# S5's rows regrouped and its small products, with one level of a block inverse, as pairs of 64x64 quadrants, in a two-layer hybrid decoder on one Trainium2 core

## Chip, cores and metric

One NeuronCore of a Trainium2 chip runs the whole program. The metric is the device time of one execution in microseconds (us), lower is better; of the kernel before there are three runs and one execution taken by the profiler.

## What is computed

Two layers of a decoder trunk on 512 tokens of width 1024, in float32. Each layer has a half-step SwiGLU feed-forward, three token mixers side by side with one input and one output projection, and a second feed-forward, each between two RMS norms. The change touches the mixer S5 and the solution of the triangular systems of the two others.

```python
def s5_mix(u, a_re, a_im, log_dt, b_re, b_im, c_re, c_im, d_skip, w_glu, b_glu):
    ug = u.reshape(bsz, t_len, S5_GROUPS, S5_GROUP_DIM)          # 16 groups x 16 channels
    dt = jnp.exp(log_dt)[:, None]
    mag = jnp.exp(dt * a_re)
    ang = dt * a_im
    abar_re, abar_im = mag * jnp.cos(ang), mag * jnp.sin(ang)    # 16 groups x 64 states
    ...
    bu_re = jnp.einsum('btgh,gnh->btgn', ug, bbar_re)
    bu_im = jnp.einsum('btgh,gnh->btgn', ug, bbar_im)
    ...
    _, _, x_re, x_im = lax.associative_scan(_complex_linear_combine, elems, axis=1)
    y = (jnp.einsum('btgn,ghn->btgh', x_re, c_re) - jnp.einsum('btgn,ghn->btgh', x_im, c_im)
         + d_skip.reshape(S5_GROUPS, S5_GROUP_DIM) * ug)
    z = jax.nn.gelu(y.reshape(bsz, t_len, S5_WIDTH))
    return z * jax.nn.sigmoid(z @ w_glu + b_glu)
...
    sol = lax.linalg.triangular_solve(a_low + eye, rhs, left_side=True, lower=True, unit_diagonal=True)
```

## The kernel before

The sequence is cut into two halves of 256 tokens (`HALF`), and `run` goes through steps such as A00 (first feed-forward, layer 0, half 0), P00 (input projection), M00 (the mixers), O00 (output projection), B00 (second feed-forward). The steps overlap: a scheduler that simulates a timeline (`schedule_with_timeline_sim`) sets the order of the instructions on each engine, so small products of a mixer stand between the large ones of a feed-forward. Each engine works through its own list in order; loads and stores are all issued by SP.

The large products are made three times (`mm3`, lines 245 to 247), from a high and a low part of each weight: `raw` is loaded by SP (line 221), ScalarE makes `whi` (line 226), VectorE makes `wlo` (line 227). `ph` are the feed-forward's up products, `acc` its down products.

S5 works in blocks of four time steps. Of the 16 groups, two (g = 0, 1) share each of 8 pairs p. In `s5_setup` (once a layer) two powers-of-Abar tables are built: `Bx` (64 states of two groups on the 128 partitions, by step and channel) and `Q` (the same for C). As two groups share a row block, the entries of one group against the other are zeros: `Bx` and `Q` are set to zero by POOL, and POOL copies each group's block into place (lines 1192 and 1220). 16 transposes (`plv`, line 1207) turn `Bx`, 16 products (`pk5`, line 1238) form the response within a block of four steps, to which VectorE adds (line 1245). All of it goes to DRAM as `s5w`. `s5` (once per half and layer, four calls) writes its input to DRAM and reads it back as `U4` with rows in the order (step, channel of the pair) by one DMA (line 1259), forms v with 16 products of 128x128 weights and 64 columns (line 1271), runs the recurrence on VectorE, and forms y with 24 products (lines 1313 to 1315).

The two other mixers need the inverses of 16 triangular 128x128 matrices in each call, 8 in `AT` and 8 in `ATg`. `inverse` inverts their 32x32 diagonal blocks by a recurrence on VectorE. `inverse2` goes from 32 to 64 and from 64 to 128: at the first level 8 products `py` (line 610) and 8 products `pz` (line 618) for each of the two groups of matrices, full 128x128 weights and 64 columns, of which half of each output is masked off or meets zeros; 16 transposes (line 625) then bring the transposed result `W` up to date. At the second level the products already are single 64x64 quadrants (lines 632 and 639). An fp32 product stands as two records in the trace, a transpose or a `mm3` product as one.

The pools that the changed tiles use are `b1`, `b2` and `b4` in SBUF and two PSUM banks `mx`. RWKV's products at line 763 are the one place where two halves of the array's rows are used in turn:

```python
for j in range(2):
    for o in (1, 0):
        q = slice(64 * o, 64 * o + 64)
        m = nc.tensor.matmul(ps[o][:, j], a[q, j, c], ar[q, j, c], start=True, stop=True)
```

Of the kernel before, what the change touches and what calls it, by code (L numbers as in the profile page):

```python
# [12 lines left out]
F32 = mybir.dt.float32  # L13
# [3 lines left out]
AF = mybir.ActivationFunctionType  # L17
ALU = mybir.AluOpType
# [23 lines left out]
class Trunk:  # L42
# [52 lines left out]
    def constants(self):  # L95
# [18 lines left out]
        self.hind = self.band(2, 64, 64, 0, "hind")  # L114
        self.bd32 = self.band(4, 32, 32, 0, "bd32")
        self.m32 = self.band(2, 32, 64, 32, "m32")
# [13 lines left out]
    def params(self, l):  # L130
# [20 lines left out]
        for s in range(4):  # L151
            self.late(nc.sync.dma_start(out=rows[R_D:R_D + 8, 32 * s:32 * s + 32],
                                        in_=io["s5_d"][l].rearrange("(p q) -> p q", q=32)))
# [430 lines left out]
    def inverse2(self, ATs, X0):  # L584
# [8 lines left out]
        nc.vector.transpose(wc.rearrange("p n k -> p (n k)"), xc.rearrange("p n k -> p (n k)"))  # L593
        Xs, Ws = [], []
        for z in range(2):
            xb = self.b4([P, 8, 4, 32], "xb")
            nc.vector.tensor_tensor(xb, xc[:, 8 * z:8 * z + 8].unsqueeze(2).to_broadcast([P, 8, 4, 32]),
                              self.bd32.unsqueeze(1).unsqueeze(3).to_broadcast([P, 8, 4, 32]), ALU.mult)
            X = xb.rearrange("p h b k -> p h (b k)")
# [3 lines left out]
            Xs.append(X)  # L603
            Ws.append(W)

        Ys = []
        for z in range(2):
            py = self.mx([P, 8, 2, 32], "py")
# [6 lines left out]
        for z in range(2):  # L615
            pz = self.mx([P, 8, 2, 32], "pz")
# [502 lines left out]
    def s5_setup(self, l):  # L1119
# [58 lines left out]
        Pw = [(self.b1([P, 8, 16], "P0r"), self.b1([P, 8, 16], "P0i"))]  # L1178
        self.cmul(Pw[0][0], Pw[0][1], b16(cr), b16(ci), Bre, Bim, [P, 8, 16])
        Cc = []  # L1180
        for cl in L["C"]:
            pc = self.mx([P, P], "pc")
            nc.tensor.transpose(pc, cl.rearrange("p t n -> p (t n)"), self.ident)
            cc = self.b1([P, 8, 16], "cc")
            nc.vector.tensor_copy(cc.rearrange("p a b -> p (a b)"), pc)
            Cc.append(cc)
        W5 = self.s5w[l]

        Bx = [self.b4([P, 8, 4, 2, 16], "Bx") for _ in range(2)]
        for t in Bx:  # L1190
            self.late(nc.gpsimd.memset(t, 0.0))
        cp = lambda o, i: nc.gpsimd.tensor_scalar(o, i, 1.0, 0.0, ALU.mult, ALU.add)
        cur = Pw[0]
        for j in range(4):
            for z in range(2):
                for g in range(2):
                    q = slice(64 * g, 64 * g + 64)
                    cp(Bx[z][q, :, 3 - j, g], cur[z][q])
            if j < 3:
                nx = (self.b1([P, 8, 16], "Pr"), self.b1([P, 8, 16], "Pi"))  # L1200
                self.cmul(nx[0], nx[1], b16(abr), b16(abi), cur[0], cur[1], [P, 8, 16])
                cur = nx
        for z in range(2):
            for hp in range(2):
                pv = self.mx([P, 4, P], "plv")
                for p in range(4):
                    nc.tensor.transpose(pv[:, p], Bx[z][:, 4 * hp + p].rearrange("n s g c -> n (s g c)"), self.ident)
                lv = self.b2([P, 4, P], "lv")
                nc.scalar.activation(lv, pv, AF.Copy)
                nc.sync.dma_start(out=W5[:, 4 * hp:4 * hp + 4, z], in_=lv)  # L1210
        Q = [[self.b4([P, 4, 5, 32], "Q") for _ in range(2)] for _ in range(2)]
        for t in Q[0] + Q[1]:
            self.late(nc.gpsimd.memset(t, 0.0))
        cur = Cc
        for j in range(5):
            for z in range(2):
                for g in range(2):
                    q = slice(64 * g, 64 * g + 64)
                    for hp in range(2):
                        nc.gpsimd.tensor_scalar(Q[z][hp][q, :, j, 16 * g:16 * g + 16], cur[z][q, 4 * hp:4 * hp + 4],  # L1220
                                                1.0 - 2 * z, 0.0, ALU.mult, ALU.add)
            if j < 4:
                nx = (self.b1([P, 8, 16], "Qcr"), self.b1([P, 8, 16], "Qci"))
                self.cmul(nx[0], nx[1], b16(abr), b16(abi), cur[0], cur[1], [P, 8, 16])
                cur = nx
        for z in range(2):
            for hp in range(2):
                nc.sync.dma_start(out=W5[:, 4 * hp:4 * hp + 4, 2 + z], in_=Q[z][hp][:, :, 1:5].rearrange("n p j c -> n p (j c)"))

        for hp in range(2):  # L1230
            pk = self.mx([P, 4, P], "pk5")
            rep = [self.b2([P, 4, 4, 32], "rep") for _ in range(2)]
            for z in range(2):
                nc.scalar.activation(rep[z], Bx[z][:, 4 * hp:4 * hp + 4, 3].rearrange("n p g c -> n p (g c)").unsqueeze(2)
                                     .to_broadcast([P, 4, 4, 32]), AF.Copy)
            for p in range(4):
                for z in range(2):
                    nc.tensor.matmul(pk[:, p], rep[z][:, p].rearrange("n s c -> n (s c)"),
                                     Q[z][hp][:, p, 0:4].rearrange("n j c -> n (j c)"), start=z == 0, stop=z == 1)
            K = self.b2([P, 4, P], "K5")  # L1240
            nc.gpsimd.tensor_tensor(K, self.ident.unsqueeze(1).to_broadcast([P, 4, P]),
                                    pr[:, R_D + 4 * hp:R_D + 4 * hp + 4].unsqueeze(2).to_broadcast([P, 4, P]), ALU.mult)
            for s in range(4):
                q = slice(32 * s, 32 * s + 32)
                nc.vector.tensor_tensor(K[q, :, 32 * s:], K[q, :, 32 * s:], pk[q, :, 0:P - 32 * s], ALU.add)
            nc.sync.dma_start(out=W5[:, 4 * hp:4 * hp + 4, 4], in_=K)


    def s5(self, l, h, I, mixT):
# [3 lines left out]
        W5 = self.s5w[l]  # L1253
# [5 lines left out]
        nc.sync.dma_start(out=U4, in_=scr.rearrange("s q p c -> (s q) p c"))  # L1259
# [6 lines left out]
        for p2 in range(4):  # L1266
            lv = self.mw.tile([P, 2, 2, P], F32, tag="lv5", name=self.n("lv5"), bufs=4)
            self.after(nc.sync.dma_start(out=lv, in_=W5[:, 2 * p2:2 * p2 + 2, 0:2]), I["usi"])
            for p in range(2):
                for z in range(2):  # L1270
                    nc.tensor.matmul(pv[z][:, 2 * p2 + p], lv[:, p, z], U4[:, 2 * p2 + p], start=True, stop=True)
# [36 lines left out]
        for p2 in range(4):  # L1308
            lx = self.b4([P, 2, 3, P], "lx5")
            self.after(nc.sync.dma_start(out=lx, in_=W5[:, 2 * p2:2 * p2 + 2, 2:5]), scan)  # L1310
            for p in range(2):
                q = 2 * p2 + p
                nc.tensor.matmul(py[:, q], lx[:, p, 2], U4[:, q], start=True, stop=False)
                nc.tensor.matmul(py[:, q], lx[:, p, 0], X[0][:, q, 0:NC5], start=False, stop=False)
                nc.tensor.matmul(py[:, q], lx[:, p, 1], X[1][:, q, 0:NC5], start=False, stop=True)
# [203 lines left out]
```

## Time and profile before

| | us |
|---|---|
| runs (median of three) | 2262.53 (2256.43 to 2264.71) |
| profiled execution | 2262.76 |
| its span, first to last instruction | 2261.0 |
| TensorE busy | 2204.1 |
| VectorE busy | 1688.2 |
| ScalarE busy | 1191.7 |
| POOL busy | 163.2 |

The profile names engines PE (TensorE's products), PEld (its weight loads), DVE (VectorE), ACT (ScalarE), POOL, SP (which issues DMAs, SPq). L763 is line 763. A name such as `pk<-ar,ka` is output from inputs, and buffer numbers are left out. 64*128 behind a product are the rows and columns of the array that it uses.

### The profile page before, as it was taken

The page shows a single profiled execution, that of the slowest core. Times are in us where ns is not written, and L with a number is a line of the kernel's source. Part 1 is how long each engine was busy: PE and PEld are TensorE (multiplying, and loading weights), DVE is VectorE, ACT ScalarE, POOL GpSimd, SP SyncE. Part 2 cuts the span into 40 slices and gives each one's busy share as a digit, 9 for nine tenths or more (in the row PEclk, how much of TensorE's full clock was granted, in tenths as well). Part 3 has the DMA queues.
Part 4 walks back from the last instruction along what each step waited for, and adds up shares of the span by engine and source line. Part 5 has one row for each costly group of instructions (what it writes and reads, how often), then busy time and mean ns, then how long its engine had stood idle before and what let it go on. Part 6 is the DMA issues. An engine that isn't in the chain of part 4 may idle for free.

```text
span 2261.0 us, 44455 instructions
## 1 busy us (share of the span) xinstructions
PE 2204.1 (97%) x15800; PEld 2032.1 (90%) x15800; DVE 1688.2 (75%) x3779; ACT 1191.7 (53%) x2521; POOL 163.2 (7%) x372
## 2 busy tenths in 40 slices
PE   8999999999999999999999999999999899998998
PEld 7998999897979999799989999889979799997997
DVE  6697886867876967768776678878677878677665
ACT  5555764444744444555555557544456545455554
POOL 2032000001000001201300010000020000001000
PEclk9999999999999999999999999999999999999999
DMA  7776765654765744567656677556467556456665
GB/s 207 199 209 186 186 196 151 187 145 153 202 192 154 206 136 142 175 186 220 200 177 188 189 197 204 155 172 189 130 179 207 162 172 193 123 154 187 190 187 154
DMA packets 604963, 403.67 MB, mean 179 GB/s; under 512 B 63306, under 2 KB 534340, under 8 KB 604740
## 3 DMA queue, kind: packets, MB, share of 16 engines
q1 hardware_dynamic: 604740, 400.82, 61.3%
q8 instruction: 124, 2.03, 0.4%
q14 instruction: 99, 0.81, 0.1%
HBM read 387.09 MB, written 13.63 MB: 177 GB/s over the span
## 4 chain that ended last, share of the span: by engine, by line
PE 87%; DVE 5%; DMA 4%; issue 1%; ACT 1%; POOL 0%; SPq 0%; DVEq 0%; ACTq 0%; POOLq 0%
PE ph L247 14%; PE ph L246 14%; PE ph L245 14%; PE acc L245 7%; PE acc L246 7%; PE acc L247 7%; PE pp L245 4%; PE pp L247 4%; PE pp L246 4%; PE acc L1386 2%; DVE wlo L227 1%; PE xt L309 1%; DMA blk<-scr 1%; PE py L610 1%; DMA raw<-in_w_in 1%
## 5 line engine op out<-in xcount | busy, mean ns | idle before, releaser
L226 ACT ACTIVATE whi<-raw 128x512 fp32r<-128x512 f32 (+2 forms) x1296 | 813.2, 632 | 835.4 <-PE ph L246 401.3
L227 DVE TENSOR_TENSOR wlo<-raw,whi 128x512 fp32r<-128x512 f32 (+2 forms) x1296 | 889.1, 690 | 408.5 <-ACT whi L226 397.2
L245 PE MATMUL ph<-hth,whi 128*128 128x256 f32 x2464 | 701.5, 285 | 6.1 <-DVE gu L364 3.2
L247 PE MATMUL ph<-hth,wlo 128*128 128x256 f32 x2464 | 702.4, 285 | 4.4 <-DVE wlo L227 4.1
L246 PE MATMUL ph<-htl,whi 128*128 128x256 f32 x2464 | 701.3, 285 | 3.9 <-DVE htl L318 3.8
L245 PEld LDWEIGHTS ph<-hth,whi 128*128 128x128 f32 x2464 | 466.6, 189 | 18.5 <-issue 3.9
L246 PEld LDWEIGHTS ph<-htl,whi 128*128 128x128 f32 x2464 | 466.2, 189 | 14.1 <-DVE htl L318 5.5
L247 PEld LDWEIGHTS ph<-hth,wlo 128*128 128x128 f32 x2464 | 467.2, 190 | 11.7 <-DVE wlo L227 7.5
L246 PE MATMUL acc<-wlo,gh 128*128 128x512 f32 x704 | 275.6, 397 | 0.0
L247 PE MATMUL acc<-whi,gl 128*128 128x512 f32 x704 | 271.1, 398 | 0.0
L245 PE MATMUL acc<-whi,gh 128*128 128x512 f32 x704 | 257.4, 400 | 0.6 <-ACT whi L226 0.6
L247 PEld LDWEIGHTS acc<-whi,gl 128*128 128x128 f32 x704 | 131.6, 188 | 29.4 <-issue 0.7
L246 PEld LDWEIGHTS acc<-wlo,gh 128*128 128x128 f32 x704 | 132.0, 188 | 23.4 <-issue 0.7
L245 PEld LDWEIGHTS acc<-whi,gh 128*128 128x128 f32 x704 | 130.3, 189 | 22.5 <-ACT whi L226 0.8
L245 PE MATMUL pp<-hth,whi 128*128 128x256 f32 x352 | 99.6, 284 | 2.8 <-ACT whi L226 2.5
L245 PE MATMUL ph<-hx,whi 128*128 128x256 f32 x352 | 99.3, 282 | 0.9 <-DVE gu L364 0.9
L370 ACT ACTIVATE gh<-gu 128x256 fp32r<-128x256 f32 x176 | 71.7, 407 | 52.6 <-DVE gu L364 51.7
L246 PE MATMUL pp<-htl,whi 128*128 128x256 f32 x352 | 98.9, 282 | 0.4 <-DVE htl L318 0.4
L247 PE MATMUL pp<-hth,wlo 128*128 128x256 f32 x352 | 99.0, 283 | 0.3 <-DVE wlo L227 0.2
L247 PE MATMUL ph<-hx,wlo 128*128 128x256 f32 x352 | 99.2, 282 | 0.0
L246 PE MATMUL ph<-hx,whi 128*128 128x256 f32 x352 | 98.8, 281 | 0.0
L245 PE MATMUL pp<-hx,whi 128*128 128x256 f32 x352 | 98.7, 281 | 0.0
(492 smaller groups left out, 3355.0 us busy)
## 6 DMA issues: line engine op xcount, KB each, us to landing
raw<-in_ffn_w SPq DMA_DIRECT2D x1056, 256.0 KB
raw<-in_w_in SPq DMA_DIRECT2D x176, 256.0 KB
raw<-in_w_out SPq DMA_DIRECT2D x96, 256.0 KB
raw<-in_w_in SPq DMA_DIRECT2D x32, 260.0 KB
gain<-in_norm_gain SPq DMA_DIRECT2D x28, 256.0 KB
lx<-s5w SPq DMA_DIRECT2D x16, 384.0 KB
lv<-s5w SPq DMA_DIRECT2D x16, 256.0 KB
x<-in_x SPq DMA_DIRECT2D x4, 512.0 KB
```

Of the source, the lines that this page charges most:

```text
L226: nc.scalar.activation(hi, q, AF.Copy)
L227: nc.vector.tensor_tensor(lo, q, hi.bitcast(F32), ALU.subtract)
L245: mm(out, lh, rh, start=start, stop=False)
L246: mm(out, lh, rl, start=False, stop=False)
L247: mm(out, ll, rh, start=False, stop=stop)
L309: self.turned = nc.tensor.transpose(pt[:, kk, i * P:(i + 1) * P], xs[i][:, k * P:(k + 1) * P], self.ident)
L370: nc.scalar.activation(gh, u, AF.Copy, scale=0.5)
L610: nc.tensor.matmul(py[:, h], ATs[z][:, h], Xs[z][:, h].rearrange("p (q e k) -> p q e k", e=2, k=32)[:, :, 0, :], start=True, stop=True)
L1386: nc.tensor.matmul(accs[i][d], mixT[:, k, s], ws[d], start=k == 0, stop=k == KT - 1)
```

## The change

Rows and columns of S5's small matrices go in the order (group, step, channel) instead of (step, group, channel). A group then has a 64x64 block of its own, and every product of two groups becomes two products on two quadrants of the array: rows 0 to 63 with columns 0 to 63, and rows 64 to 127 with columns 64 to 127. `Bx` and `Q` hold no zeros; VectorE writes them in place, and POOL's copies and memsets are gone. The tables in DRAM shrink (`s5v` with 128 and `s5w` with 192 columns for each pair and row where `s5w` had 640). U4 is read by eight DMAs and s1 written by eight. In the inverse's level 32 to 64 the products become pairs of quadrants with 32 columns, and the transposed result is formed by a product of its own (line 630 of the changed kernel) in place of the transposes.

```diff
+        self.e2 = c.tile([P, 2], F32, name="e2", tag="e2")
+        nc.gpsimd.tensor_tensor(self.e2, self.bd32[:, 0:2], self.bd32[:, 2:4], ALU.add)
...
+            xb = self.b2([P, 8, 2, 32], "xb")
+            nc.vector.tensor_tensor(xb, xc[:, 8 * z:8 * z + 8].unsqueeze(2).to_broadcast([P, 8, 2, 32]),
+                                    self.e2.unsqueeze(1).unsqueeze(3).to_broadcast([P, 8, 2, 32]), ALU.mult)
...
-                nc.tensor.matmul(py[:, h], ATs[z][:, h], Xs[z][:, h].rearrange("p (q e k) -> p q e k", e=2, k=32)[:, :, 0, :],
-                                 start=True, stop=True)
-            Y = self.b2([P, 8, 2, 32], "Y")
-            nc.vector.tensor_tensor(Y, py, self.m32.unsqueeze(1).unsqueeze(3).to_broadcast([P, 8, 2, 32]), ALU.mult)
+                for s in halves:
+                    nc.tensor.matmul(py[s, h], ATs[z][s, h, s], Xs[z][s, h, 0:32], start=True, stop=True)
+            Y = self.b1([P, 8, 32], "Y")
+            nc.vector.tensor_scalar(Y, py, self.e2[:, 1:2], None, ALU.mult)
...
-                nc.tensor.matmul(pz[:, h], Ws[z][:, h], Ys[z][:, h], start=True, stop=True)
-            xe = Xs[z].rearrange("p h (q e k) -> p (h q) e k", e=2, k=32)[:, :, 0, :]
-            nc.vector.tensor_tensor(xe, xe, pz.rearrange("p h q k -> p (h q) k"), ALU.subtract)
-        for z in range(2):
-            for g in range(2):
-                pt = self.mx([P, 4, P], "ptx")
-                for h in range(4):
-                    nc.tensor.transpose(pt[:, h], Xs[z][:, 4 * g + h], self.ident)
-                nc.scalar.activation(Ws[z][:, 4 * g:4 * g + 4], pt, AF.Copy)
+                for s in halves:
+                    nc.tensor.matmul(pz[s, h, 0], W[s, h, s], Y[s, h], start=True, stop=True)
+            for h in range(8):
+                for s in halves:
+                    nc.tensor.matmul(pz[s.start:s.start + 32, h, 1], Y[s, h], W[s, h, s.start + 32:s.stop], start=True, stop=True)
+            nc.vector.tensor_tensor(X[:, :, 0:32], X[:, :, 0:32], pz[:, :, 0], ALU.subtract)
+            for s in halves:
+                nc.scalar.activation(W[s.start:s.start + 32, :, s.start + 32:s.stop], pz[s.start:s.start + 32, :, 1], AF.Copy, scale=-1.0)
...
+        for j in (2, 1, 0):
+            self.cmul(*at(Bx, j), b16(abr), b16(abi), *at(Bx, j + 1), [P, 8, 16])
...
+            nc.vector.tensor_scalar(Q[z][:, :, 0], pc.rearrange("p (a b) -> p a b", a=8), 1.0 - 2 * z, None, ALU.mult)
...
         for j in range(4):
+            self.cmul(*at(Q, j + 1), b16(abr), b16(abn), *at(Q, j), [P, 8, 16])
...
-                        nc.gpsimd.tensor_scalar(Q[z][hp][q, :, j, 16 * g:16 * g + 16], cur[z][q, 4 * hp:4 * hp + 4],
-                                                1.0 - 2 * z, 0.0, ALU.mult, ALU.add)
...
-                    nc.tensor.matmul(pk[:, p], rep[z][:, p].rearrange("n s c -> n (s c)"),
-                                     Q[z][hp][:, p, 0:4].rearrange("n j c -> n (j c)"), start=z == 0, stop=z == 1)
+        for p in range(8):
             for z in range(2):
+                for q in halves:
+                    nc.tensor.matmul(pk[q, p], rep[z][q, p].rearrange("n s c -> n (s c)"),
+                                     Q[z][q, p, 0:4].rearrange("n j c -> n (j c)"), start=z == 0, stop=z == 1)
...
-        nc.sync.dma_start(out=U4, in_=scr.rearrange("s q p c -> (s q) p c"))
+        for g in range(2):
+            for s in range(4):
+                nc.sync.dma_start(out=U4[64 * g + 16 * s:64 * g + 16 * s + 16], in_=scr[s, 16 * g:16 * g + 16])
...
-                    nc.tensor.matmul(pv[z][:, 2 * p2 + p], lv[:, p, z], U4[:, 2 * p2 + p], start=True, stop=True)
+                    for q in halves:
+                        nc.tensor.matmul(pv[z][q, 4 * hp + p], lv[q, p, z], U4[q, 4 * hp + p], start=True, stop=True)
...
+                for k, m in ((2, U4[:, i]), (0, X[0][:, i, 0:NC5]), (1, X[1][:, i, 0:NC5])):
+                    for q in halves:
+                        nc.tensor.matmul(py[q, i], lx[q, p, k], m[q], start=k == 2, stop=k == 1)
...
-        for t in range(4):
-            nc.sync.dma_start(out=scz[t].rearrange("p q c -> q p c"), in_=s1[32 * t:32 * t + 32])
+        for g in range(2):
+            for t in range(4):
+                nc.sync.dma_start(out=scz[t, :, 16 * g:16 * g + 16].rearrange("p q c -> q p c"),
+                                  in_=s1[64 * g + 16 * t:64 * g + 16 * t + 16])
```

TensorE's order in the setup of layer 0, around `pk5`, before; `ph` are products of the feed-forward, and `Q_1829` and `rep` are S5's tables:

```order
L247 MATMUL ph_2603<-hth_170,wlo_2643 128x256
L1238 MATMUL pk_428_1919<-Q_1827,rep_1920 128x128
L245 MATMUL ph_2603<-hth_179,whi_2642 128x256
L246 MATMUL ph_2603<-htl_180,whi_2642 128x256
L247 MATMUL ph_2603<-hth_179,wlo_2643 128x256
L245 MATMUL ph_2603<-hth_183,whi_2642 128x256
L246 MATMUL ph_2603<-htl_184,whi_2642 128x256
L1238 MATMUL pk_428_1919<-Q_1829,rep_1921 128x128
```

The same place after (TensorE), and VectorE's last operations on `Q` ahead of it:

```order
L251 MATMUL ph_2531<-hth_200,whi_2540 128x256
L252 MATMUL ph_2531<-htl_201,whi_2540 128x256
L253 MATMUL ph_2531<-hth_200,wlo_2541 128x256
...
L252 MATMUL ph_2531<-htl_218,whi_2540 128x256
L253 MATMUL ph_2531<-hth_217,wlo_2541 128x256
L1222 MATMUL pk_407_1843<-Q_1769,rep_1844 64x64 x2
L1222 MATMUL pk_407_1843<-Q_1770,rep_1845 64x64 x2
```

```order
L1075 TENSOR_TENSOR cm_398_1796<-s5abn_1777,Q_1769 128x128
L233 TENSOR_TENSOR wlo_2541<-raw_2538,whi_2540 128x512
L1076 TENSOR_TENSOR Q_1769<-Q_1769,cm_397_1795 128x8x16
L369 SCALAR_TENSOR_TENSOR gu_2500<-gt_2498,ph_2425 128x256
L1077 TENSOR_TENSOR Q_1770<-Q_1770,cm_398_1796 128x8x16
```

All 32 products of `pk5` now stand together, behind the products that use `wlo_2541`, where one stood ahead of 15; their operand Q comes from VectorE.

TensorE's order in the inverse of layer 1, half 0, before (`py`, `pz`, `ptx` are the inverse's outputs; `acc` and `ph` the feed-forward's):

```order
L610 MATMUL py_19714<-xb_19700,AT_19259 128x64 x8
L246 MATMUL acc_20224<-wlo_21821,gh_21708 128x512
L610 MATMUL py_19725<-xb_19707,ATg_19437 128x64 x8
...
L618 MATMUL pz_19736<-Y_19723,W_19702 128x64 x8
L618 MATMUL pz_19746<-Y_19734,W_19709 128x64 x8
L246 MATMUL ph_21842<-htl_19099,whi_21845 128x256
...
L625 MATMUL ptx_19756<-ident,xb_19700 128x128 x4
```

and after:

```order
L618 MATMUL py_19779<-xb_19765,AT_19281 64x32 x16
L618 MATMUL py_19798<-xb_19772,ATg_19459 64x32 x16
L252 MATMUL acc_20334<-wlo_21936,gh_21817 128x512
L253 MATMUL acc_20334<-whi_21935,gl_21818 128x512
...
L253 MATMUL ph_21951<-hth_19107,wlo_21955 128x256
L627 MATMUL pz_19817<-Y_19796,W_19767 64x32 x16
L630 MATMUL pz_19817<-W_19767,Y_19796 32x32 x16
L627 MATMUL pz_19853<-Y_19815,W_19774 64x32 x16
L630 MATMUL pz_19853<-W_19774,Y_19815 32x32 x16
L639 MATMUL py_4384_19889<-xb_19765,AT_19281 64x64 x8
L251 MATMUL ph_21951<-hth_19111,whi_21954 128x256
```

7 large products stand between `py` and `pz` where 16 stood, and the first products of the second level (line 639) follow without a large one between.

SP's order where `U4` is read, layer 0, half 0, before and after (T, U and M are the recurrence's tables, `raw` weights):

```order
L221 DMA raw_6292<-in_ffn_w 128x4x128
L1259 DMA U_1081_4920<-s5u_4911 128x512
L1264 DMA T_1082_4922<-s5t_127 128x512
L1264 DMA U_1083_4923<-s5t_128 128x512
L1264 DMA M_1084_4924<-s5t_129 128x512
```

```order
L227 DMA raw_6307<-in_ffn_w 128x4x128
L1246 DMA U_1056_4848<-s5u_4839 16x512 x8
L1251 DMA T_1057_4857<-s5t_135 128x512
L1251 DMA U_1058_4858<-s5t_136 128x512
L1251 DMA M_1059_4859<-s5t_137 128x512
```

The one load became eight of 16 partitions each, at the same place.

## Rows read from the trace of the kernel before

**Rows 1.** The page, engines: busy us (share of the span) xinstructions.
```profile
PE 2204.1 (97%) x15800; PEld 2032.1 (90%) x15800; DVE 1688.2 (75%) x3779; ACT 1191.7 (53%) x2521; POOL 163.2 (7%) x372
```
**Rows 2.** Busy time by stretches: us, engines (x instructions), PEclk, DMA share, GB/s.
```profile
410.00:420.00 10.00, 10.00 (x80) 9.59 (x79) 10.00 (x28) 4.03 (x8) 0.00 (x0) 1.00 0.66 196
490.00:500.00 10.00, 10.00 (x103) 9.01 (x103) 3.92 (x7) 3.95 (x7) 0.00 (x0) 1.00 0.37 110
```
**Rows 3.** Timeline of TensorE around v: start us, us, engine, line, operation, xrecords.
```profile
390.21 0.28 PE L246 MATMUL ph<-htl,whi 128*128 128x256 f32 x1
390.33 1.89 PE L1271 MATMUL v<-U,lv 128*128 128x64 f32 x16
...
392.23 0.28 PE L245 MATMUL ph<-hth,whi 128*128 128x256 f32 x1
392.35 0.28 PE L246 MATMUL ph<-htl,whi 128*128 128x256 f32 x1
```
**Rows 4.** Timeline of TensorE around the inverse's second level, single quadrants.
```profile
820.25 0.28 PE L246 MATMUL ph<-htl,whi 128*128 128x256 f32 x1
820.46 1.14 PE L632 MATMUL py<-xb,AT 64*64 64x64 f32 x16
...
821.75 0.28 PE L245 MATMUL ph<-hth,whi 128*128 128x256 f32 x1
...
825.27 0.28 PE L246 MATMUL ph<-htl,whi 128*128 128x256 f32 x1
825.48 2.08 PE L639 MATMUL pz<-W,Y 64*64 64x64 f32 x32
...
827.70 0.28 PE L245 MATMUL ph<-hth,whi 128*128 128x256 f32 x1
```
**Rows 5.** Timeline of TensorE around RWKV's pairs of row halves.
```profile
333.63 0.28 PE L247 MATMUL ph<-hth,wlo 128*128 128x256 f32 x1
333.83 1.13 PE L763 MATMUL pk<-ar,ka 64*128 64x256 f32 x8
...
335.12 0.28 PE L246 MATMUL ph<-htl,whi 128*128 128x256 f32 x1
```
**Rows 6.** Timeline of TensorE around full-array fp32 products of 256 columns.
```profile
443.86 0.28 PE L246 MATMUL ph<-htl,whi 128*128 128x256 f32 x1
443.99 1.46 PE L1332 MATMUL pz<-zz,wglu 128*128 128x256 f32 x6
...
445.40 0.28 PE L245 MATMUL ph<-hth,whi 128*128 128x256 f32 x1
```
**Rows 7.** Timeline of TensorE around a transpose with 32-column weights.
```profile
1413.58 0.28 PE L246 MATMUL ph<-htl,whi 128*128 128x256 f32 x1
1413.70 0.27 PE L557 MATMUL pvr<-ident,vrn 128*32 128x128 f32 x1
...
1413.92 0.28 PE L245 MATMUL ph<-hth,whi 128*128 128x256 f32 x1
```
**Rows 8.** Waits of TensorE: engine, line, releaser: us in total, times, longest.
```profile
PE pk L1238 <- POOL Q L1220: 4.3, 2, 2.2
```
**Rows 9.** Timeline of TensorE at pk5, layer 0 (in brackets: idle before, releaser).
```profile
173.39 5.24 PE L1238 MATMUL pk<-Q,rep 128*128 128x128 f32 x30 [2.15 <-POOL Q L1220]
178.39 0.36 PE L247 MATMUL ph<-hth,wlo 128*128 128x256 f32 x1
```
**Rows 10.** Busy time of the stretch in pk5, with the granted clock.
```profile
176.00:178.00 2.00, 2.00 (x12) 2.00 (x10) 1.48 (x4) 0.00 (x0) 1.27 (x8) 0.50 0.68 194
```
**Rows 11.** SP's timeline at U4, and the durations of s5u's issues (min/median/max ns).
```profile
383.91 0.48 SPq L1259 DMA_DIRECT2D U<-s5u  x1
...
385.94 4.08 SPq L221 DMA_DIRECT2D raw<-in_ffn_w  x3
...
L1257 SPq DMA_DIRECT2D s5u<-us x32: 303/430/690, 290.1 to 1743.6; - x32
```

More of the change, by code (lines that the diff above doesn't have):

```diff
@@ L151, in params @@
         for s in range(4):
-            self.late(nc.sync.dma_start(out=rows[R_D:R_D + 8, 32 * s:32 * s + 32],
-                                        in_=io["s5_d"][l].rearrange("(p q) -> p q", q=32)))
+            self.late(nc.sync.dma_start(out=rows[R_D:R_D + 8].rearrange("p (g s c) -> p g s c", g=2, s=4)[:, :, s],
+                                        in_=io["s5_d"][l].rearrange("(p g c) -> p g c", g=2, c=16)))
         put(R_CONV, io["gdn_conv_w"][l].rearrange("i (t c) -> (i t) c", c=P), 48)
@@ L1182, in s5_setup @@
+        Q = [self.b4([P, 8, 5, 16], "Q") for _ in range(2)]
+        for z, cl in enumerate(L["C"]):
             pc = self.mx([P, P], "pc")
             nc.tensor.transpose(pc, cl.rearrange("p t n -> p (t n)"), self.ident)
[L1184 to L1191, printed above, removed]
@@ L1195, in s5_setup @@
             for z in range(2):
[L1196 to L1202, printed above, removed]
-        for z in range(2):
[L1204 to L1210, printed above, removed]
@@ new lines, in s5_setup @@
+                pv = self.mx([64, 4, P], "plv")
+                for p in range(4):
+                    nc.tensor.transpose(pv[:, p], Bx[z][:, 4 * hp + p].rearrange("n s c -> n (s c)"), self.ident)
+                nc.scalar.activation(lv[:, :, :, z], pv.rearrange("r p (g n) -> r p g n", g=2), AF.Copy)
+            for g in range(2):
+                nc.sync.dma_start(out=WV[64 * g:64 * g + 64, 4 * hp:4 * hp + 4], in_=lv[:, :, g])
+        for z in range(2):
+            nc.sync.dma_start(out=WX[:, :, z], in_=Q[z][:, :, 1:5].rearrange("n p j c -> n p (j c)"))
@@ new lines, in s5_setup @@
+        pk = self.mx([P, 8, 64], "pk5")
+        rep = [self.b2([P, 8, 4, 16], "rep") for _ in range(2)]
+        for z in range(2):
+            nc.scalar.activation(rep[z], Bx[z][:, :, 3].unsqueeze(2).to_broadcast([P, 8, 4, 16]), AF.Copy)
+        halves = (slice(0, 64), slice(64, P))
+        for p in range(8):
+            for z in range(2):
+                for q in halves:
+                    nc.tensor.matmul(pk[q, p], rep[z][q, p].rearrange("n s c -> n (s c)"),
+                                     Q[z][q, p, 0:4].rearrange("n j c -> n (j c)"), start=z == 0, stop=z == 1)
@@ L1265, in s5 @@
         pv = [self.mx([P, 8, NC5], "v5") for _ in range(2)]
[L1266 to L1269, printed above, removed]
+        for hp in range(2):
+            lv = self.mw.tile([P, 4, 2, 64], F32, tag="lv5", name=self.n("lv5"), bufs=4)
+            self.after(nc.sync.dma_start(out=lv, in_=WV[:, 4 * hp:4 * hp + 4]), I["usi"])
+            for p in range(4):
                 for z in range(2):
-                    nc.tensor.matmul(pv[z][:, 2 * p2 + p], lv[:, p, z], U4[:, 2 * p2 + p], start=True, stop=True)
+                    for q in halves:
+                        nc.tensor.matmul(pv[z][q, 4 * hp + p], lv[q, p, z], U4[q, 4 * hp + p], start=True, stop=True)
         Zr, Zi, t2 = self.b2([P, 8, NC5], "Zr"), self.b2([P, 8, NC5], "Zi"), self.b2([P, 8, NC5], "z2")
@@ L1307, in s5 @@
         py = self.mx([P, 8, NC5], "y5")
[L1308 to L1315, printed above, removed]
+        for hp in range(2):
+            lx = self.b4([P, 4, 3, 64], "lx5")
+            self.after(nc.sync.dma_start(out=lx, in_=WX[:, 4 * hp:4 * hp + 4]), scan)
+            for p in range(4):
+                i = 4 * hp + p
+                for k, m in ((2, U4[:, i]), (0, X[0][:, i, 0:NC5]), (1, X[1][:, i, 0:NC5])):
+                    for q in halves:
+                        nc.tensor.matmul(py[q, i], lx[q, p, k], m[q], start=k == 2, stop=k == 1)
         s1, s2 = self.b2([P, 8, NC5], "ge1"), self.b2([P, 8, NC5], "ge2")
@@ L1432, in run @@
         self.vf = [self.dr.tile([P, 2, HALF], F32, name=f"vf{h}", tag=f"vf{h}") for h in range(2)]
-        self.s5w = [self.dr.tile([P, 8, 5, P], F32, name=f"s5w{l}", tag=f"s5w{l}") for l in range(DEPTH)]
+        self.s5w = [self.dr.tile([P, 8, 3, 64], F32, name=f"s5w{l}", tag=f"s5w{l}") for l in range(DEPTH)]
+        self.s5v = [self.dr.tile([P, 8, 2, 64], F32, name=f"s5v{l}", tag=f"s5v{l}") for l in range(DEPTH)]
         s5t = [[self.dr.tile([P, 512], F32, name=f"s5t{l}{i}", tag=f"s5t{l}{i}") for i in range(3)] for l in range(DEPTH)]
```

71 lines of the change are left out of this document (27 added, 44 removed).

## Prediction

> **What bounds the kernel now.** I read the page's engine shares first [rows 1]: TensorE is busy 2204.1 of 2261.0 us, VectorE 1688.2. So a microsecond of TensorE work is worth about a microsecond, unless another engine fills the place where it goes. Then the busy time by stretches, in the places where the change works [rows 2]: while S5's second half runs (410 to 420 us) VectorE is full as well, 10.00 of 10; while the inverse ends (490 to 500) it has 3.92 of 10. A saving pays in full in the second place and only in part in the first. Last the timeline of TensorE around the small products, for what one of them costs between the large ones.
>
> The price of a product is read as the distance between the large products on either side of it. A large one takes a slot of 0.12 us (392.23 to 392.35) [rows 3]. From 390.21 to 392.23 lie two such slots and 16 records of full-array products of 64 columns: 2.02 - 0.24 = 1.78 us, **0.111 us a record** [rows 3]. An fp32 product is two records, a transpose one. With 64x64 weights, one quadrant at a time, 16 records lie within 1.50 us and 32 within 2.43 (820.25 to 821.75, 825.27 to 827.70) [rows 4]. The second 16 cost 0.93 us, **0.058 a record**, and what remains of the first 1.50 - 0.24 = 1.26 is **0.33 us for each entry into quadrants and return**.
>
> Whether two quadrants run beside one another has no row. The nearest is RWKV's pair, which puts 64 of the 128 rows of the array to one product and 64 to another [rows 5]: 8 records of 256 columns in 1.49 - 0.24 - 0.33 = 0.92 us, 0.115 each, where products over all 128 rows take (1.54 - 0.24) / 6 = 0.217 [rows 6]. So two row halves do run side by side there, and I take two quadrants with different rows and columns to do the same: 0.058 us for a pair of records. The other bound is 0.116, one after the other.
>
> **Part by part, one call of the mixers (there are four).** Before: 32 records for v, 48 for y, 32 for the inverse's first product and 32 for its second, all full-array, 144 x 0.111 = 16.0 us. Its 16 transposes I price at the same 0.111, since they load weights of the same 128 columns: 1.8. Together 17.8. After: each full record becomes a pair, 144 x 0.058 = 8.35 us. The transposes give way to 32 pairs of records with 32-column weights and 32 columns moving (line 630), for which there is no row: between half of a 64x64 slot, 0.029, and a whole one, 0.058. I take 0.035, near the lower end since both sides halve: 1.1 us. Together 9.5.
> By the Trainium skill (TensorEngine Tiling (Array Packing), Performance Considerations) a matmul has about 60 cycles of overhead and is no shorter below that, so one should not take a tiling factor from a dimension that is already small. At 2.4 GHz that would be an estimated 25 ns for each of 64 such records, 1.6 us a call instead of 1.1, and 2236.5 us in the end instead of 2234.5; no run here shows it.
>
> The orders give the entries: 13 groups of single quadrants before, 36 groups after in the four calls (two for v, three for y, one for the first product, three for the rest), so 23 x 0.33 = 7.6 us more. Within a group the width changes between 64 and 32 columns four times a call; a transpose with 32-column weights between two large products costs 0.34 - 0.24 = 0.10 us, no more than its own slot [rows 7], so I take 0 for that change and keep 0.33 as the other end (5.3 us in all). Sum of the four calls: 4 x (17.8 - 9.5) - 7.6 = **-25.6 us**.
>
> **The setup, once a layer.** Its 32 records of pk5 become 32 pairs: 32 x 0.111 = 3.55 us against 32 x 0.058 + 0.33 = 2.2; -2.7 for both layers. The second part is a wait. TensorE stood 4.3 us in front of these products for Q, which POOL copies into place [rows 8]; 30 of the records then took 173.39 to 178.39, 5.00 us instead of 30 x 0.111 = 3.33 [rows 9], because the granted clock was 0.50 in that stretch, the lower of its two levels [rows 10]. Right before it the engine had stood idle 2.15 us. VectorE now writes Q in place, and in the new order pk5 stands 12 products behind the ones that use the wlo just ahead of Q's last two operations. That is some 1.4 us of cover for about 1 us of VectorE work, so I let the wait go, and the slow stretch with it: -(4.3 + 2 x 1.67) = **-7.6 us**. The transposes of Bx stay 16, with 128 columns moving: nothing. POOL's copies and memsets go away, and VectorE's eight partial adds into K become four: nothing, since neither is waited for once Q's copies are gone.
>
> **What comes back.** (1) y saves 48 x 0.053 - 3 x 0.33 = 1.55 us a call, in the stretch where VectorE is full; I count half as lost: +3.1, between 0 and 6.2. (2) SP issues eight loads of U4 where it issued one of 0.48 us, at about 0.43 each [rows 11]: 2.96 us later for the weight loads behind them, and four more writes of s1, 1.7 us. Before, U4 was issued at 383.91 and v began at 390.33 without a wait [rows 3, 11], so most is covered: the eighth load is issued at about 387. Half a microsecond a call, +2; if the cover fails, the second rival. (3) The inverse's chain TensorE, VectorE or ScalarE, TensorE has fewer large products between its steps in the order (in one call 7 where there were 16). The next quarter's 0.9 us of products stand there as well: 0.4 a call, +1.6, between 0 and 6. (4) pk5 may still wait for VectorE: +1, between 0 and 7.6. Together +7.7.
>
> -25.6 - 2.7 - 7.6 + 7.7 = -28.2 from the profiled execution's 2262.76 us: **2234.5 us**, -1.25%. The median of the runs shown is 2262.53, 0.2 below that execution, so the same number holds for it. With nothing given back and 0.029 for the narrow pairs it is 2226; with 0.058 for them, 0.33 for each change of width, y's saving wholly lost and the setup's wait left, 2252.
>
> **The rivals.**
> *The quadrants run one after the other* (slower). In RWKV's pair the halves write two different tiles; here both write the same tile, on different partitions. If that, or the loading of the weights, makes them queue, each pair slot is 0.116 us. A call then costs 288 x 0.058 + 64 x 0.029 + 1.9 for entries = 20.5 us against 17.8, +11 for four; the setup +1; the wait of pk5 still goes (-7.6 + 1), and points (2) and (3) stay (+3.6): some +9, **2272 us**. It decides from about 0.10 us a pair on: there the gain is used up. For it: no row has two quadrants at once, nor two row halves in one tile. Against it: rows 5, where weights and columns of both halves go in side by side.
> By the Trainium skill (TensorEngine Tiling (Array Packing), Restrictions and Gotchas) different row tiles cannot access the same PSUM bank at the same time, and that speaks for this rival, although the two quadrants here differ in their columns too. Rows 5, with its halves in two tiles, cannot tell.
>
> *S5's input comes late.* The eight loads and the queue behind them aren't covered: v and the weights behind it wait 3 us a call (2.96 of issue), and the idle time brings a stretch at the lower clock as in the setup, 1.67 us. 4 x 4.7 = 18.7 instead of the 2 counted: **2251 us**. For it: SP works in order, and VectorE-bound stretches follow right behind. Against it: 6.4 us between issue and use.
>
> *Half-filled arrays lower the granted clock.* The inverse's end becomes some 4 us of quadrants in a row. Each stretch at 1.2 GHz cost 1.67 us in the setup; one or two a call are +7 to +13: **2241 to 2248 us**. Against it: at 490 to 500 us the clock stayed at 1.00 with four groups of single quadrants in it [rows 2].
>
> **How the numbers follow.** Forecast 0.62, one after the other 0.10, late input 0.12, lower clock 0.10; 0.06 for what I don't see, a stall moved elsewhere. The runs of before spread from 2256.43 to 2264.71, so 0.5%, 11.3 us, is about what a measurement here tells from no change. Faster by more than that (below 2251.2): nearly all of the forecast, the lower clock, a third of the late input: 0.75. Within it: most of the late input, half of the first rival, half of the rest: 0.17. Slower: 0.08. The range goes from 2222 (the best case less the runs' spread of 4) to 2259 (the forecast's worst, 2252, with the late input's 2251 and the spread); it leaves out the first rival and the unseen.
>
> **What would show it.** In the changed kernel's timeline: v's 31 later products as one block of 62 records within about 2 us, where two blocks of 16 took 1.8 each; the inverse's first product, 64 records, within about 2.2 us instead of 3.6. In the waits: no line of pk5 waiting for POOL, and none of v waiting for U4. In the page: two fewer stretches at the lower clock, TensorE's share still about 97%. I am wrong if blocks of quadrants last 0.1 us a pair or more, if TensorE's idle time grows by more than 10 us, or if the gain is under 11 us with short blocks: then VectorE or the weight loads bound more of the mixers than rows 2 say.

## The result, and the profile after

Before 2261.67 us, after **2233.94 us** (medians of five runs each): the ratio is 0.9887 with a 95% interval of 0.9871 to 0.9904, -27.7 us by the medians. In two later sets, with other runs of the kernel before beside it, the changed kernel was at 0.9876 (0.9861 to 0.9891) and 0.9883 (0.9860 to 0.9905), -28.8 and -26.5 us. The forecast was 2234.5.

The profiled execution took 2238.45 us, the slowest of its five. Its engines on the page, against [rows 1]:
```profile
PE 2177.7 (97%) x16632; PEld 1997.8 (89%) x16632; DVE 1666.5 (75%) x3773; ACT 1190.5 (53%) x2517; POOL 104.4 (5%) x249
```
TensorE has 26.4 us less to do and is still busy 97% of the span. The timeline of TensorE in the changed kernel (start us, us, engine, line, operation, records): v, pk5 of layer 0, the inverse's first product and the chain behind it.
```profile
388.13 0.28 PE L252 MATMUL ph<-htl,whi 128*128 128x256 f32 x1
388.34 2.08 PE L1259 MATMUL v<-U,lv 64*64 64x64 f32 x62
390.35 0.39 PE L253 MATMUL ph<-hth,wlo 128*128 128x256 f32 x1
390.57 0.28 PE L251 MATMUL ph<-hth,whi 128*128 128x256 f32 x1
...
169.32 2.08 PE L1222 MATMUL pk<-Q,rep 64*64 64x64 f32 x64
171.34 0.24 PE L131 MATMUL grt<-ident,grows 24*128 24x24 f32 x1
...
785.59 1.12 PE L618 MATMUL py<-xb,AT 64*64 64x32 f32 x32
786.54 1.10 PE L618 MATMUL py<-xb,ATg 64*64 64x32 f32 x32
787.57 0.39 PE L252 MATMUL ph<-htl,whi 128*128 128x256 f32 x1
...
789.75 1.12 PE L627 MATMUL pz<-Y,W 64*64 64x32 f32 x32
790.81 0.69 PE L630 MATMUL pz<-W,Y 64*32 64x32 f32 x32
791.43 1.12 PE L627 MATMUL pz<-Y,W 64*64 64x32 f32 x32
792.48 0.69 PE L630 MATMUL pz<-W,Y 64*32 64x32 f32 x32
793.11 1.14 PE L639 MATMUL py<-xb,AT 64*64 64x64 f32 x16
```
v's 62 records lie between two large products 2.44 us apart (388.13 to 390.57). Less their two slots and the entry that is 2.44 - 0.24 - 0.33 = 1.87 us for 31 pairs, **0.060 a pair**: two quadrants run side by side. Before, 16 records, half of v, took 1.8 [rows 3]. pk5 starts with no wait in brackets, where it stood 2.15 us [rows 9], and its 64 records take 2.0 us, where 30 of the 32 before took 5.0 at the lower clock. Each change between 64- and 32-column weights shows in the chain: 16 pair slots would be 0.92 us, and the next block starts after 1.06 or 1.05; 16 narrow pairs at the 0.0315 at which they follow each other would be 0.50, and the next starts after 0.62 or 0.63. So a change costs some **0.13 us**.

TensorE's waits in the changed kernel (engine, line, releaser: us in total, times, longest):
```profile
PE ph L253 <- DVE wlo L233: 5.3, 6, 1.5
...
PE acc L251 <- ACT gh L376: 2.0, 1, 2.0
PE py L618 <- DVE xb L604: 2.0, 2, 1.6
PE y L1303 <- DMA lx<-s5w: 1.7, 2, 1.2
...
PE py L639 <- ACT W L633: 0.9, 2, 0.5
```
pk5's line [rows 8] is gone, and v has no line for U4. The lines of gh, xb and W are new.

### The profile page after: what moved, and what is told of

Its sections match the earlier page's. It is cut to its first block, busy times and chain, and to the rows that moved or that the text cites. A ratio compares the mean times of both kernels' runs of the same rounds, so it can differ in the third digit from the quotient of the medians.

```text
span 2236.7 us, 45992 instructions
## 1 busy us (share of the span) xinstructions
PE 2177.7 (97%) x16632; PEld 1997.8 (89%) x16632; DVE 1666.5 (75%) x3773; ACT 1190.5 (53%) x2517; POOL 104.4 (5%) x249
## 4 chain that ended last, share of the span: by engine, by line
PE 87%; DVE 4%; DMA 4%; issue 2%; ACT 1%; SPq 1%; POOL 0%; DVEq 0%; ACTq 0%; POOLq 0%
PE ph L251 14%; PE ph L253 14%; PE ph L252 14%; PE acc L252 7%; PE acc L251 7%; PE acc L253 7%; PE pp L251 4%; PE pp L252 4%; PE pp L253 4%; PE acc L1376 1%; DVE wlo L233 1%; PE xt L315 1%; PE pav L795 1%; DMA raw<-in_w_out 1%; PE y L1303 1%
```

## Experiments

A run's interval is that of its ratio to the kernel before. What the small products cost is taken as in the prediction and summed over the four calls: the time from each record's start to the next record's, plus what the large products on either side of a group take beyond their usual slot (0.12 us, or 0.23 with 512 columns), less TensorE's waits. Before, that is 14.3 us for v, 22.5 for y (run 6, where none of it stands at the lower clock) and 55.1 for the inverse; in the changed kernel it is 10.6, 15.4 and 40.6. "Idle time" is the span less TensorE's busy time, both from the page.

**1 and 2. The parts alone.** Run 1 is the kernel before with the new second half of the inverse, run 2 the new kernel with the old one (its first product here):
```diff
-                for s in halves:
-                    nc.tensor.matmul(py[s, h], ATs[z][s, h, s], Xs[z][s, h, 0:32], start=True, stop=True)
+                nc.tensor.matmul(py[:, h], ATs[z][:, h], Xs[z][:, h].rearrange("p (q e k) -> p q e k", e=2, k=32)[:, :, 0, :],
+                                 start=True, stop=True)
...
```


> The kernel before with the inverse's change alone; S5 and its setup stay as they were. Theory (each part pays what its records save): 80 full-array records a call at 0.111 (8.9 us) become 64 pair slots at 0.058 and 32 narrow pairs at 0.035 (4.8 us), 3 entries more in the four calls, 1.6 us given back: -13.8 us, about 2248; pk5 still waits some 4 us for POOL's Q and still has its two stretches at the lower clock. Rival (S5's products pay nothing because VectorE is full beside them, and the whole change is the inverse and the setup's wait): then the inverse must carry about -18 us, about 2243.

> The changed kernel with the inverse as before; S5, its setup and constants as changed. Theory: 80 records a call become 80 pair slots (4 x 80 x 0.053 = 17.0), 20 entries more (-6.6), pk5's products 2.7 and its wait with the slow stretches 7.6, less 6.1 given back for y beside a full VectorE, SP and VectorE: -14.6 us, about 2247. Rival (y and v pay nothing beside a full VectorE): the setup's -10.3 alone, about 2251, and TensorE's idle time grows by some 4 us or more against the kernel before without pk5's wait. The two runs e1 and e2 should add up to the whole change (-27.7) within their intervals.

Measured: run 1 2250.15 us, 0.9942 (0.9927 to 0.9957), with pk5's 4.3 us of waiting still there; run 2 2239.42 us, 0.9890 (0.9872 to 0.9909). The inverse costs about 41 us in run 1, as in the whole change, and v and y together 26.0 in run 2, the same as there. Run 1's -11.8 by the medians is near its theory; run 2's -22.6 is 8 more than its theory's -14.6, so nothing of the 6.1 us shows that S5's part was to give back, and that theory missed. Each part pays at least about what its records save, S5 included. But by the medians they add up to -34.4, and the whole brings 6 to 8 less. Of this the profiles show a part: TensorE was busy at the lower clock for 30.1 us before, 31.5 in run 1 and 20.2 in run 2, but for 32.2, 21.9 and 29.7 in the three profiles of the changed kernel. About half of such time is loss, so some 3 us of the gap lie there. The idle time does not show the rest: 56.9 before, 65.6 in run 1, 54.5 in run 2, and 59.0, 56.7 and 54.1 in the three. A wait of 2 us for gh stands in all three and in neither part, but run 1 has 4.2 for gt and gl, other tiles of the feed-forward, instead. Why the whole brings less than its parts stays open.

**3. Quadrants apart.** In v, y and the inverse all products of one quadrant come before those of the other:
```diff
-            for p in range(4):
-                for z in range(2):
-                    for q in halves:
+            for q in halves:
+                for p in range(4):
+                    for z in range(2):
                         nc.tensor.matmul(pv[z][q, 4 * hp + p], lv[q, p, z], U4[q, 4 * hp + p], start=True, stop=True)
```


> The changed kernel, with all products of the first quadrant of a block issued ahead of those of the second, in v, y and the inverse's three products (pk5 stays in pairs). Same records, same number of entries. Theory (two quadrants run side by side only where they stand next to each other in the order): a call's 144 pair slots cost 0.116 instead of 0.058 and the 32 narrow pairs 0.07 instead of 0.035, 9.5 us a call, +38 us in four calls less up to 6 where VectorE is full: 2266 to 2272; v's block of 62 records takes about 3.9 us instead of 2.2. Rival (a quadrant's record simply costs 0.029, in whatever order, because of its size): no change, 2234, v's block 2.2 us.

Measured: 2269.06 us, 1.0030 (1.0017 to 1.0043), +35 against the changed kernel: slower than the kernel before. The timeline, with the same pairs of blocks as above:
```profile
479.07 1.84 PE L627 MATMUL pz<-Y,W 64*64 64x32 f32 x32
480.84 1.09 PE L630 MATMUL pz<-W,Y 64*32 64x32 f32 x32
481.87 1.84 PE L627 MATMUL pz<-Y,W 64*64 64x32 f32 x32
```
The same 32 records take 1.77 us, not 1.06, and 1.03, not 0.62. v is only partly apart here, 54 of its 128 pairs still starting together (15.1 us instead of 10.6); y went from 15.4 to 24.4. The size fits, but not all of it for the stated reason: TensorE was busy at the lower clock for 71.1 us instead of 32.2, which run 11 takes up.

**4 and 12. Twelve entries fewer.** v starts with the upper quadrant, and y accumulates in another order:
```diff
-                    for q in halves:
+                    for q in halves[::-1]:
                         nc.tensor.matmul(pv[z][q, 4 * hp + p], lv[q, p, z], U4[q, 4 * hp + p], start=True, stop=True)
...
-                for k, m in ((2, U4[:, i]), (0, X[0][:, i, 0:NC5]), (1, X[1][:, i, 0:NC5])):
+                for k, m in ((1, X[1][:, i, 0:NC5]), (0, X[0][:, i, 0:NC5]), (2, U4[:, i])):
                     for q in halves:
-                        nc.tensor.matmul(py[q, i], lx[q, p, k], m[q], start=k == 2, stop=k == 1)
+                        nc.tensor.matmul(py[q, i], lx[q, p, k], m[q], start=k == 1, stop=k == 2)
```


> The changed kernel with v starting with the upper quadrant (whose input is loaded last) and y accumulating X before U4: v's and y's lone first products then stand in their blocks, 12 entries into quadrants fewer in the four calls, the same records. Theory (0.33 us for each entry and return): -4.0 us, about 2230. Rival (the price is that of the first large product after a pause and is paid somewhere anyway, or v's and y's later start is waited for): no change or up to +2, 2234 to 2236.

> The kernel with 12 entries fewer once more, beside the changed kernel on one chip. Its records alone give -3.2 (v 9.0 to 8.1 us, y 12.9 to 11.7, and 12 x 0.09 for the large product ahead of each entry). Theory: -3 to -4 against the base, the -7 of its first run being stalls that fell elsewhere. Rival (the stalls that went belong to this order and stay away): -6 to -8.

Measured: 2227.04 us, 0.9841 (0.9823 to 0.9859), -6.9 against 2233.94, and beside the changed kernel of run 9 **2224.10 us**, 0.9835 (0.9814 to 0.9856): -10.8 against 2234.86, and the fastest version of all. The two intervals leave 4 to 18 us, so the rival's -6 to -8 is not excluded; the theory's -3 to -4 lies at or below their lower end. v went from 10.6 to 8.9 and y from 15.4 to 12.6, 4.5 us in all or 0.38 for each entry. The 3.2 of the expectation leaves out what the large product behind each entry costs. The two profiles are 9.0 us apart: 3.3 of the rest is idle time that is gone, 1.5 less time at the lower clock. In run 9's profile and in run 12's, the lines of y and gh:
```profile
PE acc L251 <- ACT gh L376: 2.1, 1, 2.1
PE y L1303 <- DMA lx<-s5w: 1.3, 2, 1.1
```
Run 12's list has neither. y's first product of each weight tile needed only U4, so it stood early in TensorE's order and waited there for its weights, with everything behind it. Behind X it no longer does. Why gh no longer waits was not tested.

**5 and 9. The changed kernel again**, the base of the runs beside it.

> The changed kernel itself once more, on the chip of the next three runs, as the base they are compared with: 2232 to 2238 as in its first five runs. If the stalls that are left sit at fixed places of the program, its list of waits reads as before; if they are chance, it doesn't.

> The changed kernel once more, the base of the next three runs on their chip: 2230 to 2236.

Measured: 2231.03 and 2234.86 us. The waits for gh, x, W, most of htl and lx stand in all three lists at the same places, and so does that for xb at about 467 us (1.6, 1.2 and 0.5). They belong to the order, not to chance. A second wait for xb (0.45 at 1899 us) and 2.0 us for gt stand in one list each.

**6. Only pk5's wait.** One line of the kernel before:
```diff
-                        nc.gpsimd.tensor_scalar(Q[z][hp][q, :, j, 16 * g:16 * g + 16], cur[z][q, 4 * hp:4 * hp + 4],
+                        nc.vector.tensor_scalar(Q[z][hp][q, :, j, 16 * g:16 * g + 16], cur[z][q, 4 * hp:4 * hp + 4],
```


> The kernel before with one line changed: the 40 copies a layer that put Q into place run on VectorE instead of POOL; all products stay full-array. Theory (the wait of pk5 and the two stretches at the lower clock behind it are worth 4.3 + 3.3): -7.6, about 2254, no wait of pk5 for POOL, no lower clock at 175 and 1096 us. Rival (the wait then goes to VectorE, which has 40 more operations a layer): pk5 waits as long for VectorE, no change or slower, 2262 to 2266.

Measured: 2255.72 us, 0.9981 (0.9970 to 0.9991), -4.1. pk5's wait and both stretches at the lower clock are gone, as a window in pk5 shows (us, busy of PE, PEld, DVE, ACT, POOL, clock, DMA share, GB/s):
```profile
178.00:180.00 2.00, 2.00 (x18) 1.91 (x17) 2.00 (x7) 0.62 (x2) 0.00 (x0) 1.00 0.30 106
```
The clock is 1.00 where it was 0.50 [rows 10]. But VectorE's 80 operations more come back as waits for its wlo, 8.1 us instead of 4.1:
```profile
PE ph L247 <- DVE wlo L227: 8.1, 14, 1.6
```
-7.6 + 4.0 fits the measured -4, but it is no more than a fit: over the whole span TensorE's time at the lower clock fell from 30.1 to 18.7 us, more than the two stretches at pk5. In the changed kernel VectorE writes Q in place, without these copies, and the line stands at 5.3, 3.2 and 3.4.

**7. SP's issues.** U4 by two loads instead of eight:
```diff
-            for s in range(4):
-                nc.sync.dma_start(out=U4[64 * g + 16 * s:64 * g + 16 * s + 16], in_=scr[s, 16 * g:16 * g + 16])
+            nc.sync.dma_start(out=U4[64 * g:64 * g + 64], in_=scr[:, 16 * g:16 * g + 16].rearrange("s q p c -> s q (p c)"))
```


> The changed kernel with U4 read by two DMAs a call instead of eight (the same bytes, six issues fewer on SP, some 2.2 us). Theory (SP's later issue costs half a microsecond a call): -2, about 2232. Rival (the eight issues lie wholly beside other work): no change, 2234, and the same waits.

Measured: 2231.49 us, 0.9883 (0.9867 to 0.9898), against 0.9876 for the changed kernel beside it: no change. The eight issues are covered, as far as 3 us can be told. With two, v even has a wait that it had not with eight:
```profile
PE v L1258 <- DMA U<-s5u: 2.6, 2, 1.4
```

**8. Fewer entries, and the inverse's widths grouped.** On top of run 4, the 64-column products of both halves stand ahead of the 32-column ones:
```diff
+        pzs = [self.mx([P, 8, 2, 32], "pz") for _ in range(2)]
         for z in range(2):
-            W, X, Y = Ws[z], Xs[z], Ys[z]
-            pz = self.mx([P, 8, 2, 32], "pz")
+            W, pz, Y = Ws[z], pzs[z], Ys[z]
             for h in range(8):
                 for s in halves:
                     nc.tensor.matmul(pz[s, h, 0], W[s, h, s], Y[s, h], start=True, stop=True)
+        for z in range(2):
+            W, X, Y, pz = Ws[z], Xs[z], Ys[z], pzs[z]
             for h in range(8):
```


> The run with 12 entries fewer, and in the inverse both halves' 64-column products ahead of both halves' 32-column products: one change of width a call where four stood in the chain, and a chain of 128 records instead of 144. Theory (a change of width costs some 0.14 us, what the chain's 4.28 us leave after its records: 2 x 0.92 + 2 x 0.50 + 0.93 = 3.77, over four changes): -1.3 to -1.7 against that run, about 2225.5. Rival (the change is free, and what the chain leaves is its waits for VectorE's Y and ScalarE's W): about -1 or nothing by the waits alone, with the four products' records spaced as before.

Measured: 2228.64 us, 0.9870 (0.9851 to 0.9889): not better than run 4, whose interval overlaps, nor shown to be better than the changed kernel beside it (0.9876, 2231.03), though it has run 4's 12 entries fewer as well. The expected 2225.5 was missed. The records did what was expected:
```profile
792.13 2.06 PE L627 MATMUL pz<-Y,W 64*64 64x32 f32 x64
794.12 1.20 PE L632 MATMUL pz<-W,Y 64*32 64x32 f32 x64
```
1.99 us for 32 pair slots of 1.84: one change, 0.15. What it saved went into waits: 9.4 us for wlo, where run 4 has 6.8, and 1.2 for Y, which run 4's list does not have; the idle time is 62.3 us, against 52.6 in run 4. So what fewer entries are worth in the end depends on where the waits fall.

**10. y alone apart.** The y part of run 3, all else in place.

> The changed kernel with y alone in single quadrants (within each weight tile all products of the first quadrant, then those of the second); every other product keeps its place in the order, so y takes some 9 us more of TensorE in four calls (21.9 instead of 12.9 us in the run with all quadrants apart). My term (1) (VectorE is full beside y, so that half of what TensorE saves there is lost): +4.5 against the base. Rival (TensorE alone sets the end there, and term (1) is nothing): +9.

Measured: 2244.08 us, 0.9916 (0.9897 to 0.9936): +9.2 by the medians, +7.5 by the ratios. The runs favour the rival, but their intervals leave 1 to 14 us and with it the theory's +4.5. The trace decides: y costs 24.4 us instead of 15.5, and in run 9, with y in pairs, TensorE waits for VectorE in no call between y's first product and 25 us after its last, so nothing of the saving is lost to VectorE there. The same window in run 9 and in this run:
```profile
410.00:420.00 10.00, 10.00 (x141) 9.29 (x142) 9.90 (x29) 4.82 (x9) 0.00 (x0) 1.00 0.54 165
...
410.00:420.00 10.00, 10.00 (x122) 8.76 (x121) 8.23 (x24) 3.32 (x7) 0.00 (x0) 1.00 0.63 187
```
With y in pairs VectorE is at 9.90 of 10; with y apart it falls to 8.23 while TensorE stays full. VectorE had work to do, but TensorE set the pace.

**11. The inverse alone apart.** The inverse's part of run 3.

> The changed kernel with the inverse's products alone in single quadrants, v, y and pk5 in pairs. Its records take 3.6 us more a call at the full clock (first product 3.08 instead of 1.84, the chain 2.4 more), +14.6. Theory (long stretches of half the array at work bring the lower clock, as around 470 to 492, 798 to 815, 1587 to 1604 and 1938 us of the run with all apart): further +10 to +20, so +25 to +35 against the base, with lower-clock stretches at the inverse. Rival (the clock fell there for another reason, such as the waits that run happened to have): +14.6, and no more lower-clock stretches than the base has.

Measured: 2261.46 us, 0.9999 (0.9981 to 1.0016), +26.6. Windows and timeline around the third call's chain:
```profile
1574.00:1578.00 4.00, 4.00 (x68) 3.59 (x67) 2.97 (x6) 4.00 (x11) 0.00 (x0) 1.00 0.59 183
1578.00:1586.00 8.00, 8.00 (x81) 7.31 (x81) 3.41 (x8) 1.73 (x5) 0.00 (x0) 0.51 0.44 123
1586.00:1595.00 9.00, 9.00 (x88) 8.75 (x88) 1.03 (x2) 2.29 (x5) 0.00 (x0) 0.50 0.01 2
...
1580.12 3.22 PE L627 MATMUL pz<-Y,W 64*64 64x32 f32 x32
1583.27 1.72 PE L630 MATMUL pz<-W,Y 64*32 64x32 f32 x32
```
TensorE never stopped in these windows, yet the clock fell to 0.50 behind 64 records of single quadrants and stayed there through the chain, whose first block takes 3.15 us against 1.77 at the full clock. It fell at the inverse in the three other calls too (from 479, 793, 800 and 1930 us), without idle time in the 8 us ahead. Over the span TensorE was busy 59.2 us at the lower clock instead of run 9's 29.7; counted as half, that is a loss of 14.8. The two profiled spans differ by 30.4, the idle time by 3.5, and what is left, 12.1, is about what the records cost more. The expected 14.6 for them is somewhat more; it fits that at the lower clock a block of single quadrants took 1.8 times as long and not twice (3.15 to 1.77).

## Why the prediction was right, point by point

**The pair of quadrants side by side: right**, at 0.060 against 0.058, and shown from the other side by runs 3, 10 and 11. The rival of one after the other (2272) needed what run 3 makes, products of one quadrant in a row: 2269, part of it by the lower clock. By the Trainium skill (TensorEngine Tiling (Array Packing), Restrictions and Gotchas) row tiles cannot access the same PSUM bank at once; v's block disagrees, for two quadrants that write one tile on different partitions. By the Trainium skill (TensorE: Matmul & The Clock Gate, Part 3: Packing small matmuls — row/col tiling) weights are pulled ahead of running products where the row group differs, within a window of 64, while products end in order; the 0.060 a pair agrees, but in run 3's blocks, 16 records of one quadrant and then 16 of the other, 32 took 1.77 us, or 0.055 each, so next to nothing overlapped there.

**The four calls, -25.6: right.** By the prediction's own measure v fell by 3.7, y by 7.1 and the inverse by 14.5: -25.3. S5's share is -10.8 (predicted 6.6 - 4 x 80 x 0.053 = -10.4), the inverse's -14.5 (predicted -15.2). The transposes were priced well: between the large products 0.68 - 0.24 = 0.44 us for four, 0.11 each.
```profile
489.93 0.28 PE L246 MATMUL ph<-htl,whi 128*128 128x256 f32 x1
490.05 0.60 PE L625 MATMUL ptx<-ident,xb 128*128 128x128 f32 x4
490.40 0.37 PE L247 MATMUL ph<-hth,wlo 128*128 128x256 f32 x1
490.61 0.28 PE L245 MATMUL ph<-hth,whi 128*128 128x256 f32 x1
```
One term was mis-sized, the change of width: taken as 0, it costs 0.13, sixteen times (2.1). The entry, priced at 0.33, measured 0.38 in runs 4 and 12. The narrow pairs at 0.0315 were near the 0.035 taken (0.4 us less in all); by the Trainium skill (TensorEngine Tiling (Array Packing), Performance Considerations) 64 such records would cost 1.6 us a call, an estimate, and the blocks of 0.50 show 1.0.

**The setup, -2.7 and -7.6: right.** The blocks are as long as predicted, and the wait and both slow stretches are gone at pk5, in run 6 as well. But the 3.3 us of the stretches are not shown as a gain of the whole span: others came elsewhere, and TensorE's time at the lower clock went from 30.1 us to 32.2, 21.9 and 29.7.

**What comes back, +7.7: right in size, but elsewhere.** -25.3 - 2.7 - 7.6 = -35.6 against the measured 26.5 to 28.8: 7 to 9 us came back. Term (1), half of y's saving lost, was wrong: run 10 pays in full by its trace. That VectorE was full in [rows 2] did not make it the bound; with TensorE slower VectorE's share fell. Term (2), SP, did not show (run 7). Term (3), the inverse's thinner covers, was near: 0.9, 1.0 and 0.9 us for W against 1.6. The wait for xb (2.0, 1.1 and 0.5) lies ahead of the first product and not between the chain's steps, and run 2 with the old inverse has 1.3 of it. Term (4) was nothing. What came instead were waits that were not foreseen, gh's 2.0 and xb's among them, and stretches at the lower clock in other places. The three profiled spans of the changed kernel are 11.3, 4.3 and 5.4 us longer than -35.6 would make them; 6.4, 4.1 and 1.5 of it is idle time beyond the 52.6 left without pk5's wait. Half of the time at the lower clock beyond the 23.3 left without pk5's two stretches (30.1 less 6.8) would be another 4.4, -0.7 and 3.2. Terms (1), (2) and (4), 6.1 of the 7.7, did not come, and about as much came that was not foreseen: that the sum met the result is luck in this part.

**The rivals.** The late input fell with v's missing wait. The lower clock came at the end of the changed kernel's chains in one of its three profiles (run 5, third call), behind the wait of 0.6 us for W. It came in run 11 with half the quadrants at work and no wait, and through a whole chain of pairs in the profile of run 4, behind a wait of 1.0 us for xb. In run 5 and in run 4 (timeline with the wait in brackets, then the window):
```profile
1566.67 1.24 PE L639 MATMUL py<-xb,AT 64*64 64x64 f32 x16 [0.62 <-ACT W L633]
1567.00:1571.00 4.00, 4.00 (x29) 3.88 (x28) 0.40 (x1) 1.61 (x4) 0.00 (x0) 0.57 0.16 46
...
1891.77 1.12 PE L618 MATMUL py<-xb,AT 64*64 64x32 f32 x32 [1.02 <-DVE xb L604]
1893.00:1900.00 7.00, 7.00 (x128) 6.58 (x126) 3.32 (x8) 3.18 (x8) 0.00 (x0) 0.54 0.49 153
```
Run 4's chain spread over 7.3 us instead of 4.3, in the longest but one of that kernel's four runs (2230.09; two others took 2223.6 and 2224.0).

## What to carry to other kernels

Put products of different quadrants next to each other in the order: a pair then costs one slot, and apart it costs two and can lower the clock as well. Count the entries into another tiling and the changes of width (0.33 to 0.38 and 0.13 us here), and hold early products back until their block is ready: a lone early product pays an entry and can wait at the head of the queue for its weights. Holding 12 of them back saved 4.5 us of TensorE's time here; the runs gained 7 and 11, but only 2, not clear of noise, where it was combined with another change (run 8). A full engine beside TensorE is not yet a bound: make TensorE's part longer and see whether the other's share falls.

## What the runs showed that was not expected

The granted clock fell during long runs of single quadrants with no idle time on TensorE (1578 to 1595 us in run 11), and with pairs only where a wait came first (as in runs 4 and 5). A change of weight width without a change of rows costs 0.13 us inside quadrants, while with all rows it cost no more than its slot [rows 7]. By the Trainium skill (TensorEngine Tiling (Array Packing), Key Properties) a change of tiling mode drains TensorE; the 0.38 for an entry and the 0.13 agree with that, the transpose of rows 7 shows no such price. And the parts of a change that each pay alone can bring less together, by 6 to 8 of 34 us here; stretches at the lower clock far from the edited lines are some 3 of it, and the rest stays open.
